# Layer trunk on one core: the dense product with V replaced by gathers of V's rows, beside gathers of U's rows

## The chip, the cores and the metric

One core of a Trainium2 chip. The metric is the device time of one execution in microseconds; the kernel before took 3484.92 us (median of 3 runs, 3472.05 to 3491.17). The engines are TensorE (PE, with its weight loads PEld), VectorE (DVE), ScalarE (ACT), GpSimd (POOL) and SyncE (SP). POOL, ACT and SP issue transfers; 16 transfer engines carry them.

## What is computed

Two layers over 512 tokens of width 1024, all in float32. Layer 0 mixes tokens by latent attention, layer 1 by chunked gated linear attention; each is followed by an expert retrieval (PEER): for each token 8 heads pick 16 of 16384 experts each, that is 128 rows of a table U and the same 128 rows of a table V.

```python
def one_block(xi):                      # 128 tokens
    q = (xi @ w_query).reshape(B, T, PEER_HEADS, 2, PEER_HALF)
    s = jnp.einsum('bthcd,cnd->bthcn', q, sub_keys)
    ...                                 # top 16 of each half, top 16 of the sums: idx, gate
    u = u_tab[idx]
    h = jax.nn.gelu(jnp.einsum('bthkd,btd->bthk', u, xi), approximate=False)
    w = (gate * h).astype(xi.dtype)
    return jnp.einsum('bthk,bthkd->btd', w, v_tab[idx])
```

Each row of U or V is 4 KB; for 128 tokens and 128 picks either table gives 64 MB of rows.

## The kernel before

Tokens lie in four tiles of 128; tiles 0 and 1 are group A, tiles 2 and 3 group B. A tile of a layer goes through mixer (`mla` or `gla`), `router` (query product, top 16, `idx` and `gate`, in four quarters of two heads), U rows (`weigh`), and V rows.

**U rows.** `weigh` (L481) takes one pick k at a time: `gather` (L473) issues one indirect transfer on POOL at L475, one row of U for each of the 128 tokens, 512 KB, into a row buffer; VectorE multiplies it with the token's normed input and sums (L487). Row buffers come from `row` (L467), round robin: 10 of a pool, and, in the sparse stretches, further ones cut out of the tile `W` (`spare`).

**V rows, two ways.** Tiles 2 and 3 of both layers: `gathered` (L517) turns picks to lie along partitions, so one indirect transfer brings the 128 rows of V of one token; `at` (L528) is the list of rows, `wd` (L535) the weights of 16 tokens spread over columns, and L543 contracts rows with weights on TensorE, 2 tokens in 8 matmuls; halves of 64 tokens are copied out (L548) and added to `h` (L549). Tiles 0 and 1 of both layers: `combine` (L593) is a dense product with the whole of V. `spread` (L556) makes a 0/1 selection on VectorE (L569, L572, L575), TensorE builds a weight matrix from it in four quarters (L581), ScalarE copies it out (L584), and SP loads all of V in 128 blocks of 512 KB (L602), each contracted with the weights of both tiles (L605); the sums are added to `h` at L617.

**What sets the order.** The program is written as generators that yield an estimate of their cost; `mix` takes the one that is furthest behind its share. A scheduler then fixes each engine's order from this, with `urgent` parts first. Each engine runs its instructions in that order; POOL's gathers wait in turn on eight counters, so that eight at most are in flight. After the attention of all tiles, `trunk` (mixers, routers, dense product) runs against `tables` (U and V rows): `tables` fetches U of (0, 2) and (0, 3), gathers V of both, then U of all four tiles of layer 1, then V of (1, 2) and (1, 3); here (l, b) is layer and tile.

## Time and profile before

| | |
|---|---|
| median of 3 runs | 3484.92 us |
| profiled execution, its own time | 3496.72 us |
| its span | 3495.0 us |
| TensorE, mean granted clock | 0.833 |
| bytes moved | 1048.11 MB, 300 GB/s over the span |

How to read it. The table of stages gives the busy time of each engine in a stretch with the number of its instructions in brackets, then the granted TensorE clock, the mean busy share of the transfer engines and what they moved. The groups of instructions give the mean of one and the idle time ahead of them with what ended it. A timeline gives each instruction's start and length, and in square brackets how long its engine had been idle and what released it. On POOL an instruction's time is the issuing of a transfer, not the transfer.

### The profile page before, as it was taken

What the parts mean: (1) busy time and instruction counts of PE and PEld (TensorE: products, weight loads), DVE (VectorE), ACT (ScalarE), POOL (GpSimd) and SP (SyncE); (2) the same over time, 40 slices, a digit from 0 to 9 for tenths busy, and PEclk for the clock granted to TensorE, in tenths of its full rate; (3) what the DMA queues carried; (4) which work ended last, traced back from release to release, by engine and by line L of the source; (5) the groups of instructions that cost most, each with busy time, mean ns of one, the idle gap of its engine ahead of it and who ended that gap; (6) DMA issues with size and microseconds to landing.
All of it is one profiled execution on the core that took longest, in us unless ns stands there. A gap on an engine that the chain in (4) does not pass through costs nothing.

```text
span 3495.0 us, 43793 instructions
## 1 busy us (share of the span) xinstructions
PE 2672.3 (76%) x15940; PEld 1642.8 (47%) x15940; DVE 2054.9 (59%) x5744; ACT 683.1 (20%) x1736; POOL 1841.9 (53%) x1540
## 2 busy tenths in 40 slices
PE   6755378858999889997895577406399997999866
PEld 4635356744555553335575455405255553533211
DVE  1588997699998850000117987899999873200000
ACT  6463377211111110003013211002111110100000
POOL 0176776155555645553404566875876464242265
PEclk8868688957999889999997687756599998899978
DMA  4599998668888989998836789997899888587698
GB/s 142 179 373 350 332 351 310 214 215 330 311 309 295 346 279 409 390 388 314 315 107 222 273 336 335 377 351 260 266 370 333 306 307 325 199 309 263 213 374 320
DMA packets 291274, 1048.11 MB, mean 300 GB/s; under 512 B 33377, under 2 KB 34913, under 8 KB 291058
## 3 DMA queue, kind: packets, MB, share of 16 engines
q0 software_dynamic: 221184, 805.40, 62.5%
q1 hardware_dynamic: 40210, 139.50, 11.0%
q10 hardware_dynamic: 29664, 100.41, 8.4%
q8 instruction: 125, 2.05, 0.2%
q14 instruction: 91, 0.75, 0.1%
HBM read 1043.09 MB, written 2.10 MB: 299 GB/s over the span
## 4 chain that ended last, share of the span: by engine, by line
PE 48%; DVE 21%; issue 12%; DMA 7%; ACT 6%; POOL 3%; another core or an unknown queue 3%; ACTq 0%; POOLq 0%; SPq 0%; DVEq 0%
PE acc L605 21%; DVE row L487 10%; PE sp L581 8%; PE mm L543 7%; PE mm L156 6%; DMA row<-in_u,idx 3%; POOL row L475 2%; DVE W L487 2%; DVE a L569 2%; DMA W<-in_v,at 1%; PE mm L396 1%; DMA row<-in_v,at 1%; DMA W<-in_u,idx 1%; POOL W L475 1%
## 5 line engine op out<-in xcount | busy, mean ns | idle before, releaser
L475 POOL DMA_INDIRECT row<-in_u,idx x927 | 1226.1, 1323 | 839.7 <-DVE idx L456 229.1
L487 DVE SCALAR_TENSOR_TENSOR row<-row,xnf 128x1024 f32<-128x1024 f32 x927 | 1111.6, 1216 | 42.5 <-DMA row<-in_u,idx 39.6
L605 PE MATMUL acc<-V,W 128*128 128x512 f32 x2048 | 1002.6, 640 | 9.8 <-DMA V<-in_v 7.6
L605 PEld LDWEIGHTS acc<-V,W 128*128 128x128 f32 x2048 | 404.4, 206 | 518.3 <-issue 503.6
L581 PE MATMUL sp<-bw,a 128*128 128x32 bf16 x6144 | 426.1, 242 | 270.7 <-DVE bw L575 109.6
L581 PEld LDWEIGHTS <-a 128*128 128x128 bf16 x6144 | 413.3, 157 | 366.8 <-issue 229.6
L475 POOL DMA_INDIRECT row<-in_v,at x373 | 360.0, 965 | 368.2 <-PE mm L543 239.9
L584 ACT ACTIVATE W<-sp 128x256 f32<-128x256 f32 x256 | 157.7, 616 | 1063.2 <-PE sp L581 855.2
L535 DVE TENSOR_TENSOR wd<-wT,same 128x512 f32<-128x512 f32 x32 | 22.0, 691 | 558.0 <-PE mm L543 362.7
L569 DVE TENSOR_TENSOR a<-rows,iotat 128x1024 bf16<-128x1024 bf16 x256 | 175.7, 687 | 238.8 <-PE sp L581 189.1
L543 PE MATMUL mm<-row,wd 128*32 128x512 f32 x1492 | 265.5, 624 | 50.7 <-DMA row<-in_v,at 35.4
L156 PE MATMUL mm<-ws,xT 128*128 128x128 f32 (+1 forms) x1920 | 253.9, 294 | 20.5 <-issue 13.2
L156 PEld LDWEIGHTS mm<-ws,xT 128*128 128x128 f32 x1920 | 244.1, 208 | 39.4 <-issue 27.8
L475 POOL DMA_INDIRECT W<-in_v,at x139 | 132.3, 952 | 231.1 <-PE acc L605 131.3
L475 POOL DMA_INDIRECT W<-in_u,idx x97 | 123.4, 1272 | 198.2 <-issue 143.6
L543 PE MATMUL mm<-W,wd 128*32 128x512 f32 x556 | 130.2, 658 | 41.0 <-issue 28.6
L543 PEld LDWEIGHTS mm<-row,wd 128*32 128x32 f32 x1492 | 49.4, 110 | 206.1 <-issue 169.7
L396 PE MATMUL mm<-xTf,ws 128*128 128x128 f32 x1024 | 139.8, 300 | 7.2 <-ACT qTf L399 5.3
L396 PEld LDWEIGHTS mm<-xTf,ws 128*128 128x128 f32 x1024 | 136.9, 216 | 10.9 <-ACT qTf L399 5.9
L575 DVE TENSOR_TENSOR bw<-e,parts 128x768 bf16<-128x768 bf16 x256 | 139.6, 550 | 0.0
L487 DVE SCALAR_TENSOR_TENSOR W<-W,xnf 128x1024 f32<-128x1024 f32 x97 | 115.8, 1215 | 3.4 <-DMA W<-in_u,idx 3.3
L402 PE MATMUL mm<-skT,qTf 128*128 128x256 f32 x128 | 40.4, 439 | 73.1 <-ACT qTf L399 58.3
(244 smaller groups left out, 2397.6 us busy)
## 6 DMA issues: line engine op xcount, KB each, us to landing
V<-in_v SPq DMA_DIRECT2D x256, 512.0 KB
ws<-in_w_query ACTq DMA_DIRECT2D x56, 512.0 KB
ws<-in_w_in ACTq DMA_DIRECT2D x48, 512.0 KB
row<-in_u,idx POOLq DMA_INDIRECT x927
ws<-in_m_w_o ACTq DMA_DIRECT2D x24, 512.0 KB
ws<-in_g_w_o ACTq DMA_DIRECT2D x16, 512.0 KB
ws<-in_w_down ACTq DMA_DIRECT2D x15, 512.0 KB
ws<-in_w_uq ACTq DMA_DIRECT2D x24, 288.0 KB
```

What stands on the lines that cost most here:

```text
L156: nc.tensor.matmul(ps, xT[:, k, :], w[:, k, :], start=(k == 0), stop=(k == kc - 1))
L396: nc.tensor.matmul(ps[:, i * P : (i + 1) * P], w[i][:, k, :], xT[b][:, k, :], start=(k == 0), stop=(k == KC - 1))
L402: nc.tensor.matmul(ps[:, i * 256 : (i + 1) * 256], qT[:, i, :], skT[l], start=True, stop=True)
L475: nc.gpsimd.indirect_dma_start(out=t, out_offset=None, in_=tab, in_offset=bass.IndirectOffsetOnAxis(ap=idx[:, k : k + 1], axis=0))
L487: nc.vector.scalar_tensor_tensor(t, t, 1.0, xn, op0=ALU.mult, op1=ALU.mult, accum_out=dots[:, k : k + 1])
L535: nc.vector.tensor_tensor(wd, w[:, s0 : s0 + TS, :].unsqueeze(3).broadcast_to([P, TS, 2, TG]), same[:, s0 : s0 + TS, :].unsqueeze(2).broad ...
L543: nc.tensor.matmul(acc[g : g + TG, :], wd[:, s, c, :], rw[c][:, n * 512 : (n + 1) * 512], start=(s0 + s == 0), stop=(s0 + s == TG - 1))
L569: nc.vector.tensor_tensor(a2, rows[:, 1, ts_].unsqueeze(1).broadcast_to([P, NK, BT]), vp_["iota"], op=ALU.is_equal)
L575: nc.vector.tensor_tensor(bw, e1.unsqueeze(1).broadcast_to([P, 3, QB, BT]), parts[:, :, ts_].unsqueeze(2).broadcast_to([P, 3, QB, BT]), op ...
L581: nc.tensor.matmul(ps[:, t * QB : (t + 1) * QB], a2[:, :, t], bw[:, j, :, t], start=(j == 0), stop=(j == 2))
L584: nc.scalar.activation(wq[:, :, o : o + BT].rearrange("p j t -> p t j"), ps.rearrange("p (t j) -> p t j", t=BT), AF.Copy)
L605: nc.tensor.matmul(acc[b, n], wq[:, c, i * P : (i + 1) * P], vt[:, n * 512 : (n + 1) * 512], start=(q + c == 0), stop=(q == NQ - 1 and c = ...
```

## The change

`combine`, `spread`, `prefill` and `in_parts` are gone, with V's dense blocks and the selection tiles. All eight (layer, tile) pairs go through `gathered`. `tables` runs three stretches: V of (0, 0), (0, 1) beside U of (0, 2), (0, 3) at shares 2 to 1; V of (0, 2), (0, 3) beside U of (1, 0), (1, 1) at 1 to 1; U of (1, 2), (1, 3) beside V of layer 1's four tiles. A generator that has nothing ready now yields `None` and is passed over in `mix`. The row pool has 16 buffers in place of 10 after the attention, and six spare ones beside the mixer's arena, 22 in all; 9 during the attention. The normed input `xnf` has three buffers.

```diff
-ROW_D, ROW_S, SPB = 1.85, 1.5, 1.65
-NROW = 10
+ROW, SPB = 1.42, 1.65
+NROW, MROW = 9, 16
...
-            xn[b] = rp.tile([P, D], F32, tag="xn", name="xnf", bufs=2)
+            xn[b] = rp.tile([P, D], F32, tag="xn", name="xnf", bufs=3)
...
-        i = turn[0] % (NROW + len(spare))
+        i = turn[0] % ((MROW if spare else NROW) + len(spare))
...
     def mix(*gens):
         live = [[g, n, 0] for g, n in gens]
         while live:
-            s_ = min(live, key=lambda z: z[2] / z[1])
-            try:
-                c = next(s_[0])
+            late = []
+            for s_ in sorted(live, key=lambda z: z[2] / z[1]):
+                try:
+                    c = next(s_[0])
+                except StopIteration:
+                    live.remove(s_)
+                    break
+                if c is None:
+                    late.append(s_)
+                    continue
                 s_[2] += c
+                for z in late:
+                    z[2] = max(z[2], s_[2] / s_[1] * z[1])
                 yield c
-            except StopIteration:
-                live.remove(s_)
+                break
+            else:
+                yield None
...
     def trunk():
-        yield from prefill(0, A)
-        yield from mix((combine(0, A), TM), (route(0, [3]), 0.6 * TM))
-        sparse_open(W_GLA)
+        spares(W_GLA)
         gla_s["gw"] = Arena()
         free[:] = [f"acc{i}" for i in range(4)]
-        yield from chain(onward(1, A), urgent(route(1, A)))
-        yield from chain(onward(1, B), urgent(route(1, [2])))
...
-        yield from prefill(1, A)
-        yield from mix((combine(1, A), TM), (urgent(route(1, [3])), 0.2 * TM))
-        sparse_open(0)
+        yield from urgent(route(0, [3]))
+        for group in (A, B):
+            yield from until(lambda: all((0, b) in summed for b in group))
+            yield from urgent(linear(group))
+            yield from urgent(route(1, group if group is A else group[:1]))
+        yield from urgent(route(1, B[1:]))
 
     def tables():
-        yield from chain(fetch(0, B), gathered(0, 2), gathered(0, 3))
-        yield from chain(fetch(1, A), fetch(1, B), gathered(1, 2), gathered(1, 3))
+        yield from mix((chain(gathered(0, 0), gathered(0, 1)), 2), (fetch(0, B), 1))
+        yield from mix((chain(gathered(0, 2), gathered(0, 3)), 1), (fetch(1, A), 1))
+        yield from mix((fetch(1, B), 1), (chain(*[gathered(1, b) for b in A + B]), 1))
```

POOL's order where the attention ends. In the names, `row` is a buffer of the row pool, `W` a spare one; `in_u` and `in_v` are the tables, `idx` and `at` the lists of rows. Before:

```order
6 L475 DMA row<-in_u,idx 128x1024 x505
7 L475 DMA W<-in_v,at 128x1024
8 L475 DMA row<-in_u,idx 128x1024 x7
9 L475 DMA row<-in_v,at 128x1024 x5
10 L475 DMA W<-in_v,at 128x1024
```

and now:

```order
6 L475 DMA row<-in_u,idx 128x1024 x256
7 L475 DMA row<-in_v,at 128x1024 x2
8 L475 DMA W<-in_v,at 128x1024 x4
9 L475 DMA row<-in_u,idx 128x1024
10 L475 DMA row<-in_v,at 128x1024 x2
11 L475 DMA row<-in_u,idx 128x1024
12 L475 DMA row<-in_v,at 128x1024
```

After 256 U rows (tiles 0 and 1) there came 256 more; now six V rows, then two V rows to one U row for 378 gathers.

POOL's order now, round the end of U of tile 3, layer 0 (the 128 U rows before), and the first U rows of layer 1:

```order
307 L475 DMA row<-in_u,idx 128x1024 x14
308 L475 DMA W<-in_v,at 128x1024 x2
309 L475 DMA row<-in_v,at 128x1024
310 L475 DMA W<-in_v,at 128x1024 x3
311 L475 DMA row<-in_v,at 128x1024 x15
312 L475 DMA W<-in_v,at 128x1024 x3
313 L475 DMA row<-in_v,at 128x1024
314 L475 DMA W<-in_v,at 128x1024 x3
315 L475 DMA row<-in_u,idx 128x1024 x2
316 L475 DMA row<-in_v,at 128x1024 x2
```

Between the last V row of tile 1 and the first U row of layer 1 (row 315) POOL has 128 U rows and 29 V rows.

POOL's order now, from the last U row of layer 1's tile 1 to the first of its tile 2:

```order
565 L475 DMA row<-in_u,idx 128x1024 x2
566 L475 DMA row<-in_v,at 128x1024 x25
567 L475 DMA W<-in_v,at 128x1024 x6
568 L475 DMA row<-in_v,at 128x1024 x16
569 L475 DMA W<-in_v,at 128x1024 x6
570 L475 DMA row<-in_v,at 128x1024 x5
571 L475 DMA W<-in_v,at 128x1024 x6
572 L475 DMA row<-in_v,at 128x1024 x26
573 L475 DMA W<-in_v,at 128x1024 x6
574 L475 DMA row<-in_v,at 128x1024 x4
575 L475 DMA W<-in_v,at 128x1024 x3
576 L475 DMA row<-in_u,idx 128x1024
```

103 V rows of tile 0, layer 1, stand between the two. The program's last 150 gathers are V rows alone.

VectorE's order now, where the last U row of tile 3, layer 0, has been weighed (L498 closes the tile):

```order
1274 L744 COPY_PREDICATED at_5303<-keep,mm 128x128
1275 L485 SCALAR_TENSOR_TENSOR row,dots<-row,xnf 128x1024 x12
1276 L498 TENSOR_TENSOR dots<-dots,gate 128x128
1277 L749 SCALAR_TENSOR_TENSOR W<-state_5311,W,mm 128x256
1278 L749 SCALAR_TENSOR_TENSOR state_5311<-W,mm 128x256
```

The mixer of layer 1 stands there between the U rows (L485 was L487); before, its first half stood beside V rows alone.

## Rows read from the trace of the kernel before

**Rows 1.** Page, costliest groups: busy us, mean ns of one, idle before.

```profile
L475 POOL DMA_INDIRECT row<-in_u,idx x927 | 1226.1, 1323 | 839.7 <-DVE idx L456 229.1
L487 DVE SCALAR_TENSOR_TENSOR row<-row,xnf 128x1024 f32<-128x1024 f32 x927 | 1111.6, 1216 | 42.5 <-DMA row<-in_u,idx 39.6
L605 PE MATMUL acc<-V,W 128*128 128x512 f32 x2048 | 1002.6, 640 | 9.8 <-DMA V<-in_v 7.6
L581 PE MATMUL sp<-bw,a 128*128 128x32 bf16 x6144 | 426.1, 242 | 270.7 <-DVE bw L575 109.6
L475 POOL DMA_INDIRECT row<-in_v,at x373 | 360.0, 965 | 368.2 <-PE mm L543 239.9
...
L569 DVE TENSOR_TENSOR a<-rows,iotat 128x1024 bf16<-128x1024 bf16 x256 | 175.7, 687 | 238.8 <-PE sp L581 189.1
```

**Rows 2.** Table of stages: stretch, engines' busy us (instructions), clock, transfer share, GB/s.

```profile
156.00:605.00 449.00, 282.20 (x1473) 213.92 (x1474) 396.47 (x1124) 246.87 (x766) 325.14 (x254) 0.76 0.93 343
...
1833.00:1876.00 43.00, 31.78 (x232) 30.64 (x233) 23.22 (x142) 19.09 (x43) 0.00 (x0) 0.88 0.31 93
...
3170.00:3291.00 121.00, 121.00 (x317) 48.19 (x310) 2.29 (x4) 0.00 (x0) 8.45 (x9) 1.00 0.53 185
3291.00:3478.00 187.00, 119.65 (x454) 24.86 (x453) 8.73 (x12) 2.37 (x4) 121.86 (x128) 0.78 0.95 360
3478.00:3495.00 17.00, 10.06 (x74) 3.51 (x73) 1.22 (x1) 1.18 (x2) 1.07 (x2) 0.98 0.39 147
```

**Rows 3.** Timelines of POOL and VectorE: start us, us, engine, line, idle before.

```profile
1645.41 0.94 POOL L475 DMA_INDIRECT W<-in_v,at  x1 [0.30 <-issue]
...
2821.85 1.22 DVE L487 SCALAR_TENSOR_TENSOR row<-row,xnf 128x1024 f32<-128x1024 f32 x1
...
2822.47 1.40 POOL L475 DMA_INDIRECT row<-in_u,idx  x1 [2.45 <-DVE e L572]
```

**Rows 4.** Transfer view, 1340 to 1440 us in 40 slices.

```profile
GB/s 410 411 408 413 408 408 401 410 410 411 411 408 410 410 408 411 410 410 411 403 410 410 410 410 408 408 387 225 288 282 318 305 383 408 419 416 403 415 408 408
```

**Rows 5.** Timeline of VectorE, 681 to 2213 us: indices, sums, decay, states.

```profile
681.56 0.18 DVE L456 SCALAR_TENSOR_TENSOR idx<-sel 128x32 int32<-128x32 bf16 x1
...
1567.84 0.69 DVE L617 TENSOR_TENSOR h<-h,acc 128x512 f32<-128x512 f32 x1 [0.17 <-PE acc L605]
...
1614.60 0.69 DVE L787 SCALAR_TENSOR_TENSOR W<-mm,W 128x512 f32<-128x512 f32 x1 [4.30 <-ACT W L785]
...
1744.96 0.48 DVE L826 SCALAR_TENSOR_TENSOR state<-W,mm 128x256 f32<-128x256 f32 x1 [2.84 <-PE mm L831]
...
1788.12 0.48 DVE L826 SCALAR_TENSOR_TENSOR state<-W,mm 128x256 f32<-128x256 f32 x1 [4.73 <-PE mm L831]
...
1798.23 0.48 DVE L826 SCALAR_TENSOR_TENSOR state<-W,mm 128x256 f32<-128x256 f32 x1
...
1832.45 0.69 DVE L174 TENSOR_TENSOR h<-h,mm 128x512 f32<-128x512 f32 x1 [3.11 <-PE mm L156]
...
1875.35 0.18 DVE L456 SCALAR_TENSOR_TENSOR idx<-sel 128x32 int32<-128x32 bf16 x1
...
1977.99 0.68 DVE L787 SCALAR_TENSOR_TENSOR W<-mm,W 128x512 f32<-128x512 f32 x1
...
2043.49 0.47 DVE L826 SCALAR_TENSOR_TENSOR state<-W,mm 128x256 f32<-128x256 f32 x1
...
2095.45 0.48 DVE L826 SCALAR_TENSOR_TENSOR state<-W,mm 128x256 f32<-128x256 f32 x1 [1.10 <-PE mm L831]
...
2212.20 0.68 DVE L174 TENSOR_TENSOR h<-h,mm 128x512 f32<-128x512 f32 x1
```

**Rows 6.** Timelines of POOL and VectorE at the program's end.

```profile
3297.92 0.94 POOL L475 DMA_INDIRECT W<-in_v,at  x1 [5.11 <-DVE at L528]
...
3478.43 0.94 POOL L475 DMA_INDIRECT W<-in_v,at  x1 [0.30 <-issue]
...
3490.12 1.22 DVE L549 TENSOR_TENSOR h<-h,W 64x1024 f32<-64x1024 f32 x1 [20.02 <-ACT W L548]
```

More of the change, by code (lines that the diff above doesn't have):

```diff
@@ L477, in gather @@
         return t
-    dense = []
     def weigh(l, b, xn, idx, gate, sel):
@@ L488, in weigh @@
                                            accum_out=dots[:, k : k + 1])
-            yield ROW_D if dense else ROW_S
+            yield ROW
         fetched.add((l, b))
@@ L544, in gathered @@
                                              start=(s0 + s == 0), stop=(s0 + s == TG - 1))
-                    yield 2 * (ROW_D if dense else ROW_S)
+                    yield 2 * (ROW)
             o = row()
@@ L552, in tile_trunk @@
     done, fetched, routed, summed = {}, set(), set(), set()
-    wqs, split, sps = {}, {}, []
-    def spread(l, group, q):
-        wq = vp_["W"][:, (q + 1) % 2]
-        wqs[l, group[0]].append(wq)
-        for b in group:
-            if q == 0:
-                while (l, b) not in fetched:
-                    yield 0.5
-                split[l, b] = in_parts(l, b)
-            rows, parts = split[l, b]
-            for t0 in range(0, P, BT):
-                ts_ = slice(t0, t0 + BT)
-                a2 = vp_["o"].tile([P, NK, BT], BF, tag="a2", name="a2", bufs=3)
-                nc.vector.tensor_tensor(a2, rows[:, 1, ts_].unsqueeze(1).broadcast_to([P, NK, BT]), vp_["iota"],
-                                        op=ALU.is_equal)
-                e1 = vp_["o"].tile([P, QB, BT], BF, tag="e1", name="e1", bufs=3)
-                nc.vector.tensor_tensor(e1, rows[:, 0, ts_].unsqueeze(1).broadcast_to([P, QB, BT]),
-                                        vp_["iota"][:, q * QB : (q + 1) * QB, :], op=ALU.is_equal)
-                bw = vp_["o"].tile([P, 3, QB, BT], BF, tag="bw", name="bw", bufs=3)
-                nc.vector.tensor_tensor(bw, e1.unsqueeze(1).broadcast_to([P, 3, QB, BT]),
-                                        parts[:, :, ts_].unsqueeze(2).broadcast_to([P, 3, QB, BT]), op=ALU.mult)
-                sps.append(sps.pop(0))
-                ps = sps[-1]
-                for t in range(BT):
-                    for j in range(3):
-                        nc.tensor.matmul(ps[:, t * QB : (t + 1) * QB], a2[:, :, t], bw[:, j, :, t],
-                                         start=(j == 0), stop=(j == 2))
-                o = (b - group[0]) * P + t0
-                nc.scalar.activation(wq[:, :, o : o + BT].rearrange("p j t -> p t j"),
-                                     ps.rearrange("p (t j) -> p t j", t=BT), AF.Copy)
-                yield SPB
@@ L588, in prefill @@
-    def prefill(l, group):
-        wqs[l, group[0]] = []
-        yield from spread(l, group, 0)
-    def combine(l, group):
-        acc = {(b, n): vp_["ps"].tile([P, 512], F32, tag=f"acc{2 * i + n}", name="acc")
-               for i, b in enumerate(group) for n in range(2)}
-        def blocks(q, wq):
-            for c in range(QB):
-                r0 = (q * QB + c) * P
-                vt = vp_["g"].tile([P, D], F32, tag="V", name="V", bufs=3)
-                nc.sync.dma_start(vt, v_tab[l][r0 : r0 + P, :])
-                for i, b in enumerate(group):
-                    for n in range(2):
-                        nc.tensor.matmul(acc[b, n], wq[:, c, i * P : (i + 1) * P],
-                                         vt[:, n * 512 : (n + 1) * 512], start=(q + c == 0),
-                                         stop=(q == NQ - 1 and c == QB - 1))
-                yield 1.72 * len(group)
-        w = wqs[l, group[0]]
-        dense.append(l)
-        ns, nb = len(group) * P // BT * SPB, QB * 1.72 * len(group)
-        for q in range(NQ):
-            yield from mix((blocks(q, w[q]), nb), *([(urgent(spread(l, group, q + 1), SOON), ns)] if q + 1 < NQ else []))
-        for b, n in acc:
-            hs = h[b][:, n * 512 : (n + 1) * 512]
-            nc.vector.tensor_tensor(hs, hs, acc[b, n], op=ALU.add)
-        summed.update((l, b) for b in group)
-        dense.clear()
@@ L621, in dense_open @@
     def dense_open():
         vp_["ps"] = ctx.enter_context(tc.tile_pool(name="ps", bufs=1, space=PSUM))
-        t = vp_["ps"].tile([P, 2, BT * QB], F32, name="sp")
-        sps.extend(t[:, i] for i in range(2))
-        vp_["g"] = ctx.enter_context(tc.tile_pool(name="gb", bufs=NROW))
+        vp_["g"] = ctx.enter_context(tc.tile_pool(name="gb", bufs=MROW))
         w = ctx.enter_context(tc.tile_pool(name="w", bufs=1))
@@ L629, in dense_open @@
         vp_["o"] = ctx.enter_context(tc.tile_pool(name="o", bufs=2))
-        t = vp_["o"].tile([P, NK, BT], BF, name="iotat", bufs=1)
-        nc.vector.tensor_copy(t, iota.unsqueeze(2).broadcast_to([P, NK, BT]))
-        vp_["iota"] = t
     def mix(*gens):
@@ L656, in fetch @@
             while (l, b) not in routed:
-                yield 0.5
+                yield None
             yield from weigh(l, b, *picks[b])
```

29 lines of the change are left out of this document (6 added, 23 removed).

## Prediction

> **What bounds the kernel now.** I read the table of stages first [rows 2], then the groups of instructions [rows 1], then the waits. Two stretches are the dense product of V (the rows of L605 and L581). The last stretch is half empty: between 3170 and 3291 us the V gathers stop, POOL is busy 8.45 of 121 us and the transfer engines stand at 0.53, because VectorE sits in order behind the end of the dense product. Everywhere else the rows of U and V come through one queue, GpSimd's (POOL), one 512 KB gather at a time, each row at L475. So three things can set the pace there: POOL's issuing, the transfer engines, and whoever frees the rows.
>
> POOL: a gather takes 0.94 us and the next one starts 0.30 us later [rows 3], 1.24 us in all. V gathers stay there in the mean (965 ns), U gathers do not (1323 ns) [rows 1]. Why is seen at 2822.47 us: the gather begins while VectorE's multiply of a U row (L487, 1216 ns) is running, and takes 1.40 us; it ends at 2823.87, 0.80 us after the multiply's end (2821.85 + 1.22 = 2823.07) [rows 3]. So a U row costs POOL 1.323 + 0.30 = 1.62 us, a V row 0.965 + 0.30 = 1.265 us. Transfer engines: where they are full they move 408 to 413 GB/s [rows 4], 524288 B in 1.28 us. That is within 2% of POOL's price of a V row and 21% below that of a U row: in a mix POOL, not the transfers, is the pacer.
>
> **What is removed.** 256 loads of V (134 MB), the 2048 matmuls of L605 (1002.6 us of TensorE), the 6144 of L581, and on VectorE L569 (175.7 us) with its two neighbours L572 and L575 [rows 1]. What replaces them is 512 more gathers, 268 MB: the total rises by 134 MB. None of the removed work is worth its busy time; it is worth the time at which the gathers run without it.
>
> **The new order, step by step.** The order of POOL's 2048 gathers is fixed in the program (the rows of order ahead show its three turns; the counts below are from it). Until the first U row of tile 2, layer 0, nothing moves: that row waits for its index at 681.56 us [rows 5], and in between only six V rows are new. I keep 682 us; one row buffer fewer there (9 for 10) I cost at nothing, since eight gathers are in flight at most by the counters they wait on.
> 1. 378 gathers, 250 of V (tiles 0, 1) and 128 of U (tile 2): 250 x 1.265 + 128 x 1.62 = 524. At the start seven quarters of routing stand on VectorE among the first 18 U rows. A quarter costs 12 us there (23.2 us for two in the stretch 1833 to 1876) [rows 2], so 84 + 18 x 1.3 = 107 us, in which POOL gets 54 rows and some 20 buffers on: a loss of 20. Where V goes to a new tile, its list of rows (`at`, one buffer) waits for the last gather of the old one; before it cost 5.11 us in POOL's row at 3297.92 [rows 6]; three U rows cover some of it: 6. End: 682 + 20 + 524 + 6 = 1232.
> 2. Layer 1's mixer of tiles 0 and 1 can start when their V rows are summed, 12 us after the last gather (3478.43 to 3490.12) [rows 6]: 1244. It runs beside 128 U rows (tile 3) and 29 V rows, 128 x 1.62 + 29 x 1.265 = 245 us of POOL. Then POOL's next instruction is a U row of layer 1, whose index needs the mixer and the router. The leg was, before: 47 us from the sum to the decay (1567.84 to 1614.60), 218 from there to the new h under V rows, 234 under U rows (1977.99 to 2212.20), and 43 from h to the first index (1832.45 to 1875.35) [rows 5]. With U rows beside it I take 47 + 234 + 43 = 324: 1568. POOL is ready at 1477 and stands 91 us.
> 3. 489 gathers, 256 U (layer 1, tiles 0 and 1) and 233 V: 256 x 1.62 + 233 x 1.265 = 710, and 10 for routing and the change of tile: 2288. V's last row of tile 3 lies 32 gathers earlier (26 of them U, 50 us), so the second mixer starts at 2288 - 50 + 12 = 2250.
> 4. Its leg, beside V rows: 47 + 218 + 43 = 308, so 2558. POOL has only 103 V rows for it, 130 us, and 182 us if the 54 MB of rows and the 21 MB of weights fill the transfer engines. It stands some 90 us again.
> 5. 509 gathers, 256 U and 253 V: 735, with 15 for routing and 8 for the lists: 3316. Then 150 V rows alone. Before, 128 of these took 187 us [rows 2], 1.461 each: 219, so 3535. From the last gather to the end 17 us [rows 2]: 3552.
> The profiled span was 3495.0, so +57 us, 1.6%. Its execution was 3496.7 and the median of three 3484.9; I put the difference on the median: **3542 us**.
>
> What the change saves is there (no dense product, no gap before 3291) but is paid for twice: 512 more gathers at 1.27 to 1.62 us, and two legs of some 300 us on the path, each with work for POOL for only 180 to 245. A 1% change of the price of a mixed row moves the result by 20 us, and break-even lies at 1.39 us for the mean of the three mixed stretches (57 us over 1376 gathers), where I have 1.43.
>
> **A rule weighed.** At 2822.47 the gather was late by what was left of one multiply [rows 3], and in the mean a U gather is late by 0.36 us of a multiply of 1.22 [rows 1]. The Trainium skill (SBUF — State Buffer, "SBUF: two separate sides") has VectorE and GpSimd take the shared port pair as an exclusive lock for a whole instruction, so that the loser fully blocks. The trace agrees on the single instruction. If every multiply shut POOL out for its whole length, a U row would cost 1.265 + 1.216 = 2.48 us; the stretch of U alone from 156 to 605 us shows 449 / 254 = 1.77 with everything in it [rows 2], so the mean goes by the row.
> The same skill (DMA: Bandwidth & Descriptors, "Where 436 GB/s comes from") says that about 358 GB/s of HBM per core binds. The trace does not agree: 410 [rows 4]. By 358 a gather could not be under 1.46 us.
>
> **Rivals.**
> - The transfers pace, not POOL. If U and V rows mixed leave the multiplies time to fall beside POOL's pauses, every stretch goes at 1.28 us: 484 for 524, 626 for 710, 652 for 735, 192 for 219, together 234 less: 3308. For it: from 156 to 605 us, with U rows alone, the transfer engines stood at 0.93 [rows 2]; against: weights went through them there too, and POOL's mean over U rows is 1.323 [rows 1]. Chance 0.11.
> - The legs shrink. In the first mixer one head followed the other by 43 us while V rows were in TensorE's queue (state at 1744.96 and 1788.12) and by 10 once they were gone (1798.23) [rows 5]. If the first leg, which has few V rows, lost most of this, and the second some, 100 us go: 3442. Against: with U rows two heads were 52 us apart (2043.49, 2095.45) [rows 5]. Chance 0.14.
> - The slow side: POOL's rows cost what the whole stretches show, waits for late multiplies and late matmuls included: 1.77 for U (156 to 605) and 1.461 for V [rows 2]. Then step 1 is 592, step 3 793, step 5 823, +239: 3781. It decides wherever a row buffer comes back late, and 22 buffers are 30 us of slack. Against: those U rows ran beside VectorE work at 88% of the time. Chance 0.07.
> - The lock in full: 0.86 us more on 640 U rows on the path, +550: 4092. Chance 0.02.
> - My sum, with the prices of a mixed row between 1.36 and 1.50 and the legs +-25 us: 3450 to 3640. Chance 0.66.
>
> **How the numbers follow.** About 0.5% (17 us) is what a measurement of this kernel can tell from no change. Faster, under 3467: 0.11 + 0.14 + 0.02 of my own case, 0.27. Within: 0.13 of my case. Slower, over 3502: 0.51 + 0.07 + 0.02, 0.60. The range leaves out the first rival (0.11) and the two on the slow side (0.09): 3400 to 3690.
>
> **What would show it.** Right: POOL's gathers at 1.36 to 1.45 us in the two-table stretches with the transfer engines under 0.95 full; POOL standing 60 to 120 us before the first U row of layer 1 and again before that of tile 2; a last stretch of V alone at about 1.4. Wrong: full transfer engines (410 GB/s) through the mixed stretches; no stand of POOL at those two places; or stands of POOL for row buffers, named after VectorE's multiply or V's matmul, spread over the mixed stretches.

## The result, and the profile after

In the batch that timed both kernels the changed one took 3620.39 us (median of 4, 3612.01 to 3630.81) and the one before 3487.19 (3472.05 to 3491.17): a ratio of 1.0391, 95% interval 1.0356 to 1.0427. The forecast had the direction right, and its range holds the time; its size was off: 57 us more were forecast, 133 measured. A later batch with the same two kernels gave 1.0093 (1.0058 to 1.0128). Both results hold, and telling why they differ is most of what follows.

The stages of the changed kernel by the table of windows (columns: stretch in us, its length, busy us and instructions of each engine, granted clock of TensorE, busy share of the transfer engines, GB/s). The first, third and fifth are the stretches of mixed rows, the second and fourth the mixers from the decay to the new h, the sixth V rows alone, the last the end:

```profile
668.00:1222.00 554.00, 329.87 (x1087) 54.73 (x1087) 231.90 (x690) 15.46 (x37) 411.33 (x379) 0.74 0.96 361
1253.00:1550.00 297.00, 197.36 (x1274) 154.13 (x1273) 160.41 (x306) 31.07 (x74) 167.35 (x138) 0.78 0.81 302
1591.00:2314.00 723.00, 355.99 (x1110) 69.10 (x1109) 394.53 (x992) 40.18 (x80) 542.16 (x488) 0.65 0.95 356
2303.00:2579.00 276.00, 239.49 (x1592) 162.37 (x1592) 40.51 (x98) 32.11 (x76) 108.61 (x110) 0.90 0.75 272
2624.00:3377.00 753.00, 388.41 (x1044) 50.80 (x1042) 386.90 (x960) 11.66 (x25) 573.42 (x508) 0.63 0.95 353
3379.00:3592.00 213.00, 141.12 (x553) 33.24 (x554) 12.26 (x18) 2.96 (x6) 142.03 (x149) 0.80 0.96 368
3592.00:3610.00 18.00, 10.99 (x56) 3.86 (x55) 1.22 (x1) 1.18 (x2) 0.94 (x1) 0.71 0.41 166
```

These answer to [rows 2]. The dense product is gone, and with it the half-empty stretch before 3291. The two legs are read on VectorE's timeline, as in [rows 5]: the last sum of V (L533), the second decay (L710), the new h (L174), the first index (L456). Here the first leg (with its last two rows from further on), then the second:

```profile
1227.31 1.22 DVE L533 TENSOR_TENSOR h<-h,row 64x1024 f32<-64x1024 f32 x1 [0.70 <-ACT row L532]
1253.42 0.69 DVE L710 SCALAR_TENSOR_TENSOR W<-mm,W 128x512 f32<-128x512 f32 x1 [2.42 <-issue]
1549.76 1.29 DVE L174 TENSOR_TENSOR h<-h,mm 128x512 f32<-128x512 f32 x2 [6.90 <-PE mm L156]
1590.28 0.18 DVE L456 SCALAR_TENSOR_TENSOR idx<-sel 128x32 int32<-128x32 bf16 x1
...
2271.89 1.22 DVE L533 TENSOR_TENSOR h<-h,row 64x1024 f32<-64x1024 f32 x1
2302.94 0.69 DVE L710 SCALAR_TENSOR_TENSOR W<-mm,W 128x512 f32<-128x512 f32 x1 [3.73 <-issue]
2579.05 0.69 DVE L174 TENSOR_TENSOR h<-h,mm 128x512 f32<-128x512 f32 x1 [3.11 <-PE mm L156]
2623.53 0.18 DVE L456 SCALAR_TENSOR_TENSOR idx<-sel 128x32 int32<-128x32 bf16 x1
```

363 us (1227.3 to 1590.3) and 352 us (2271.9 to 2623.5). POOL's timeline shows what hangs on them: its queue stands at the first U row of layer 1, and again at the first of tile 2:

```profile
1590.73 0.94 POOL L475 DMA_INDIRECT row<-in_u,idx  x1 [65.61 <-DVE bf L447]
2623.98 1.00 POOL L475 DMA_INDIRECT row<-in_u,idx  x1 [81.83 <-DVE a L444]
```

That much was foreseen. What was not is in TensorE's list of waits (line and what it waited for: us, times, longest):

```profile
PE mm L527 <- issue: 201.7, 198, 5.3
PE mm L156 <- issue: 58.7, 50, 3.2
```

"Issue" is time in which the engine waited for nothing that the profile shows: 260 us of it, before V's matmuls and the mixer's. The same list of the kernel before has far less:

```profile
PE mm L543 <- issue: 43.1, 55, 2.2
PE mm L156 <- issue: 13.2, 22, 1.1
```

On the timeline of TensorE in the first leg such a stand looks like this:

```profile
1319.16 0.27 PE L156 MATMUL mm<-ws,xT 128*128 128x128 f32 x1 [0.33 <-issue]
1320.58 0.56 PE L156 MATMUL mm<-ws,xT 128*128 128x128 f32 x1 [1.15 <-issue]
1322.67 0.37 PE L156 MATMUL mm<-ws,xT 128*128 128x128 f32 x1 [1.53 <-issue]
1324.10 0.37 PE L156 MATMUL mm<-ws,xT 128*128 128x128 f32 x1 [1.06 <-issue]
1326.89 0.37 PE L156 MATMUL mm<-ws,xT 128*128 128x128 f32 x1 [2.42 <-issue]
1329.69 0.37 PE L156 MATMUL mm<-ws,xT 128*128 128x128 f32 x1 [2.43 <-issue]
```

The matmuls start 1.42, 2.09, 1.43, 2.79 and 2.80 us apart, about 2, 3, 2, 4 and 4 times 0.70. None is missing from the record: the mixer's matmuls of this line number 1024 in each leg of both kernels. From 1315 to 1353 only 33 of them run. The granted clock there is 0.56, but a matmul still takes 0.37 us, so the clock does not make the gaps. I call this a stand of TensorE below.

TensorE is not alone in it. POOL's list of waits in the result has 85.5 us that end by "remote", that is by no instruction on record:

```profile
POOL W L475 <- remote: 48.1, 22, 5.5
POOL row L475 <- remote: 37.4, 23, 5.2
```

The kernel before has 32.2 us of them.

### The profile page after: what moved, and what is told of

It is laid out like the page before. It is cut to its first block, busy times and chain, and to the rows that moved or that the text cites. A ratio compares the mean times of both kernels' runs of the same rounds, so it can differ in the third digit from the quotient of the medians.

```text
span 3610.2 us, 31336 instructions
## 1 busy us (share of the span) xinstructions
PE 2179.7 (60%) x9796; PEld 944.7 (26%) x9796; DVE 1781.7 (49%) x4999; ACT 528.4 (15%) x1489; POOL 2300.4 (64%) x2052
## 3 DMA queue, kind: packets, MB, share of 16 engines
q8 instruction: 77, 1.26, 0.1%
## 4 chain that ended last, share of the span: by engine, by line
issue 19%; PE 12%; DMA 10%; POOL 10%; DVE 5%; another core or an unknown queue 0%; ACT 0%; POOLq 0%; ACTq 0%; DVEq 0%
POOL row L475 7%; PE mm L527 7%; DMA row<-in_v,at 5%; PE mm L156 3%; POOL W L475 3%; DMA row<-in_u,idx 2%; DMA W<-in_v,at 2%; DMA W<-in_u,idx 1%; DVE row L485 1%; PE mm L396 1%; DVE W L485 0%; DVE tiu L370 0%; DVE s L368 0%; DVE tiu L367 0%
## 5 line engine op out<-in xcount | busy, mean ns | idle before, releaser
L527 PE MATMUL mm<-row,wd 128*32 128x512 f32 x2972 | 1007.2, 850 | 780.5 <-DMA row<-in_v,at 606.5
L475 POOL DMA_INDIRECT row<-in_u,idx x816 | 972.6, 1192 | 617.6 <-issue 201.8
L485 DVE SCALAR_TENSOR_TENSOR row<-row,xnf 128x1024 f32<-128x1024 f32 x816 | 982.8, 1221 | 569.6 <-DMA row<-in_u,idx 422.8
L475 POOL DMA_INDIRECT row<-in_v,at x743 | 797.4, 1073 | 362.7 <-issue 191.5
L527 PEld LDWEIGHTS mm<-row,wd 128*32 128x32 f32 x2972 | 144.2, 127 | 1560.9 <-DMA row<-in_v,at 1025.4
L527 PE MATMUL mm<-W,wd 128*32 128x512 f32 x1124 | 387.5, 823 | 209.5 <-DMA W<-in_v,at 147.5
L475 POOL DMA_INDIRECT W<-in_v,at x281 | 301.4, 1073 | 211.0 <-PE mm L527 94.5
L485 DVE SCALAR_TENSOR_TENSOR W<-W,xnf 128x1024 f32<-128x1024 f32 x208 | 252.0, 1224 | 140.6 <-DMA W<-in_u,idx 120.4
L156 PE MATMUL mm<-ws,xT 128*128 128x128 f32 (+1 forms) x1920 | 263.6, 297 | 58.7 <-issue 58.2
L475 POOL DMA_INDIRECT W<-in_u,idx x208 | 228.8, 1100 | 101.3 <-issue 50.6
L156 PEld LDWEIGHTS mm<-ws,xT 128*128 128x128 f32 x1920 | 251.9, 212 | 81.0 <-issue 77.0
L527 PEld LDWEIGHTS mm<-W,wd 128*32 128x32 f32 x1124 | 57.8, 128 | 461.0 <-DMA W<-in_v,at 270.0
L485 DVE DVE_READ_ACCUMULATOR row<-row,xnf 128x1 f32 x816 | 66.4, 81 | 0.2 <-issue 0.2
L156 PE MATMUL mm<-ws,oT 128*128 128x128 f32 x512 | 61.5, 279 | 6.1 <-DMA ws<-in_m_w_o 4.0
L156 PEld LDWEIGHTS mm<-ws,oT 128*128 128x128 f32 x512 | 59.3, 194 | 8.3 <-DMA ws<-in_m_w_o 4.7
```

The costliest lines, as they stand in the source:

```text
L156: nc.tensor.matmul(ps, xT[:, k, :], w[:, k, :], start=(k == 0), stop=(k == kc - 1))
L475: nc.gpsimd.indirect_dma_start(out=t, out_offset=None, in_=tab, in_offset=bass.IndirectOffsetOnAxis(ap=idx[:, k : k + 1], axis=0))
L485: nc.vector.scalar_tensor_tensor(t, t, 1.0, xn, op0=ALU.mult, op1=ALU.mult, accum_out=dots[:, k : k + 1])
L527: nc.tensor.matmul(acc[g : g + TG, :], wd[:, s, c, :], rw[c][:, n * 512 : (n + 1) * 512], start=(s0 + s == 0), stop=(s0 + s == TG - 1))
```

## Two conditions: the same kernels, with and without TensorE's stands

Kernels of one batch ran on one chip, and the kernel before was timed in each. It tells two sorts of batch apart: it takes 3479 to 3487 us, the result among them, or 3369. I name them by what their profiles show, **with stands** and **without**.

The first repetition of both kernels (no edit):

> The changed kernel as it is, once more. In its first profile TensorE stood 202 us in front of the matmuls of V rows and 59 us in front of the mixer's, waiting for nothing that the profile shows; in the kernel before these were 43 and 13 us, and in the four experiments so far none. Theory A (the stands belong to that run, not to the kernel's order): here they are under 20 us, the mixed stretches take some 1.38 us a row, the legs some 315 and 300 us, and the kernel is 0.5 to 2% slower than the one before, about 1.6% as forecast. Theory B (they belong to the kernel): 150 us or more of such stands, legs of 350 us or more, and 3 to 4.5% slower.

> The kernel before as it is, for its profile beside the others of this call. Theory A: no stands of TensorE without a cause, its V rows alone at the end at 1.27 to 1.30 us each, where its first profile had 1.46 in the whole stretch. Theory B: some 40 to 70 us of such stands as in the first profile, V rows alone at 1.4 or more.

This batch fell without stands. Changed kernel 3395.23 us, before 3368.69, ratio 1.0093 (1.0058 to 1.0128). TensorE's issue waits in the changed kernel are down to one, and the kernel before has no row of them:

```profile
PE mm L527 <- issue: 0.5, 1, 0.5
```

The same stages of the changed kernel in this batch (mixed, mixer, mixed, mixer, mixed, V alone):

```profile
667.00:1183.00 516.00, 304.12 (x1087) 48.46 (x1081) 230.47 (x688) 15.42 (x37) 396.72 (x379) 0.82 1.00 387
1214.00:1466.00 252.00, 184.94 (x1273) 147.15 (x1273) 161.61 (x306) 30.97 (x74) 163.63 (x135) 0.85 0.92 356
1505.00:2193.00 688.00, 361.06 (x1153) 70.61 (x1153) 395.10 (x996) 43.01 (x86) 538.59 (x489) 0.66 0.98 374
2180.00:2413.00 233.00, 221.04 (x1591) 147.38 (x1591) 40.56 (x98) 32.15 (x77) 109.07 (x111) 0.99 0.86 323
2458.00:3173.00 715.00, 378.43 (x1043) 48.87 (x1041) 391.43 (x962) 11.90 (x25) 555.77 (x510) 0.63 0.98 373
3173.00:3370.00 197.00, 145.61 (x577) 23.21 (x577) 12.47 (x20) 2.95 (x6) 140.29 (x149) 0.91 1.00 396
```

Every stage is shorter: the mixed ones by 38, 35 and 38 us, the mixers by 45 and 43, the end of V alone by 16. The program and POOL's order are the same. POOL has no wait for "remote" any more, in either kernel. Theory A is borne out, with the loss near the low end of its 0.5 to 2%. In its single run before_again took 3367.59 us (span 3365.8, against 3495.0) with 1.31 us a row for its last 128 V rows, where it had 1.46, so the kernel before gains 129 us of span and the changed one 224.

The unedited kernel again, in later batches:

> The changed kernel as it is, a third time, as the one to compare with in this call. If TensorE's stands without a recorded cause come and go with the run, this shows either none and a span near 3386, or more than 150 us of them and one near 3610.

> The changed kernel as it is, to see what holds in this call. Theory: the two outcomes go with the chip, which the kernel before tells too: near 3370 us it has none of TensorE's stands and the changed kernel is near 3390; near 3485 us it has some 60 us of them and the changed kernel 200 or more, near 3620. Rival (they go with the single run): a mixture, the one without the other.

3640.12 us where the kernel before took 3485.41 (median), and 3605.64 where it took 3478.82; L527 stood 165.0 and 164.5 us on issue, L156 35.9 and 37.1, and POOL's waits for "remote" were 81.6 and 85.9 us. So the stands come in every batch in which the kernel before is the slower one, and in no other: they go with the batch, and as a batch is one chip, probably with the chip (13, in two batches, and 14 with stands, 4 and 7 without; the result's is not on record). They are no chance of a single run.

What the stands need, in a batch that has them:

```diff
# e9_half: half of each row gathered, used twice
+        n //= 2
         t = row()[:, :n]
# e10_split: each matmul of a V row in two of 256 columns
-  matmul(acc[g:g+TG, :], wd[:, s, c, :], rw[c][:, n*512:(n+1)*512], ...)
+  for q in range(2):
+    matmul(acc[g:g+TG, q*256:(q+1)*256], wd[:, s, c, :], rw[c][:, n*512+q*256 : n*512+(q+1)*256], ...)
```

> The changed kernel with gathers of half a row (2 KB of 4 KB of each row), the first half multiplied or contracted twice; it leaves the other half of U and V out. As many gathers and TensorE instructions, half the bytes. Theory (TensorE's stands need full transfers): where the changed kernel shows them, they are under 30 us here. Rival (they go with the number of its instructions): they stay over 150 us. In any case the mixed stretches show POOL's own price with a half multiply: 1.25 to 1.30 us a row if POOL paces at 0.94 + 0.30.

> The changed kernel with each matmul of a V row cut in two of 256 columns, twice as many TensorE instructions for the same rows. Theory (the stands are a shortage of instructions at TensorE): where the changed kernel shows 200 us of them, 350 or more here, and the kernel is 100 us longer; where it shows none, none here and within 40 us of it. Rival (they go with the bytes or the time): as many as in the changed kernel, and within 40 us of it.

TensorE's issue waits before V's matmuls in its list of waits, all of one batch. The unedited kernel, after_fourth:

```profile
PE mm L527 <- issue: 164.5, 204, 5.7
```

With half rows, e9_half (V's matmuls stand one line lower there):

```profile
PE mm L528 <- issue: 239.9, 260, 3.2
```

With the matmuls split, e10_split:

```profile
PE mm L528 <- issue: 387.0, 426, 3.8
```

Half the bytes (183 to 187 GB/s in the mixed stretches, transfer engines at 0.63 to 0.64; the kernel took 3575.60 us) take nothing away: full transfers are not the cause. The price that I had named for that run, 1.25 to 1.30 us a row, did not come either: its second and third mixed stretch cost 1.43 and 1.44. Twice the matmuls of V rows bring 2.4 times the stands there (387.0 to 164.5), so in this order they grow with the number of TensorE's instructions; the kernel took 3673.28 us, 68 more than its neighbour, where I had expected 100. The number alone does not set them, though: e8_sixteen below has the same instructions and fewer row buffers, and 91.3 us for 165.0. A shortage of instructions is thus not shown, and what makes TensorE and POOL stand in some batches stays open. The page's row of instruction transfers reads `q8 instruction: 77, 1.26` (packets, MB) for the changed kernel in both conditions, at 0.1 and 0.2% of the transfer engines' time, so more of them is not what differs.

## The legs: what lengthens them

```diff
# e2_quiet: the rows that ran beside a leg are gathered after it (tables(), same rows in all)
+  mix(((V00, V01), 2), (fetch(0, [2]), 1));  fetch(1, [0])
+  mix(((V02, V03), 2), (fetch(0, [3]) then fetch(1, [1]), 2));  fetch(1, [2])
+  mix((fetch(1, [3]), 1), (all V of layer 1, 3))
# e3_nomul03: multiply of U rows of tile 3, layer 0, over 8 columns
+  n = 8 if (l, b) == (0, 3) else D
```

(V02 stands for gathered(0, 2), and so on.) Both without stands.

> The changed kernel with the gathers that stand beside the two legs moved behind them: the next gather of POOL is in both cases a row that needs the leg's result, so a leg runs with nothing beside it. Theory (what runs beside a leg makes it long: VectorE's multiplies in front of its steps, V rows in TensorE's queue, and a TensorE clock that falls while it waits): from the last sum of V (L533) to the first index 220 us or less, against 363 and 352 in the changed kernel, TensorE's clock 0.9 or more in the leg; POOL stands all of it, so the whole is longer, some 3780. Rival (the leg's own chain of steps is that long): 330 us or more in the quiet too, and some 4000 for the whole.

> The changed kernel in which the multiply of U rows of tile 3, layer 0, which run beside the first leg, takes 8 of 1024 columns; the gathers stay. It leaves out most of these 128 dot products. Theory A (VectorE's queue holds the first leg up: the multiplies stand in front of its steps, TensorE waits and loses its clock): the first leg falls from 363 us to 310 or less. Theory B (full transfers or TensorE's own queue hold it up): it stays at 345 or more. The second leg stays at 352 by both.

**e2_quiet**: 3652.93 us (3780 expected, by prices with stands). From sum to index 217 us (1198.95 to 1416.43) and 224 us, for 220 or less. The two mixers, decay to h, with nothing beside them:

```profile
1222.00:1377.00 155.00, 150.53 (x1164) 133.18 (x1164) 24.31 (x72) 28.45 (x70) 0.00 (x0) 0.99 0.34 103
2362.00:2518.00 156.00, 151.99 (x1163) 134.47 (x1164) 24.33 (x72) 28.00 (x69) 0.00 (x0) 0.98 0.33 102
```

TensorE is busy 97% at a granted clock of 0.99 and 0.98, and the two are alike. In the changed kernel without stands they take 252 and 233, the first at a granted clock of 0.85: what runs beside a mixer costs it 77 to 97 us. That something beside a leg makes it long holds; which of the theory's three causes it is, this run can't tell.

**e3_nomul03**: the first leg took 317 us, between the two bounds (310 or less, 345 or more), which I had set from the result's 363. The second leg, which the edit doesn't touch and which should have stayed at 352, fell to 300 as well: this batch was without stands, where the unedited kernel's legs are 317 and 307 us. So 128 multiplies less on VectorE moved the first leg by nothing that shows, and theory A falls. Only the untouched leg told this; the edited place alone, 363 to 317, would have seemed to speak for theory A.

Depth of the pool, one part of the change undone, then more:

```diff
-NROW, MROW = 9, 16
+NROW, MROW = 9, 10     # e8_sixteen: 16 buffers in all; e6_few has 6: 12 in all
```

> The changed kernel with 6 instead of 16 buffers beside the 6 spare ones, 12 for the 22. Theory (eight gathers are in flight at most and a row is free some 2 us after it landed, so 12 are enough but for blocks behind the routing and the mixer's steps): up to 60 us longer, all of it in the legs and in the first rows after them. Rival (the 22 carry the mixed stretches): 1.55 us a row or more in the mixed stretches, 150 us longer.

> The changed kernel with 10 instead of 16 buffers beside the 6 spare ones, 16 for the 22: the part of the change that adds buffers is undone. Theory (a deeper pool lets more landed rows queue in front of the mixer's steps on VectorE and TensorE): the legs lie between those with 22 (317 and 307 us) and with 12 (284 and 272), the span between 3386 and 3336, about 3365. Rival (with 12 the order of the program merely fell better): no shortening, 3386 or more.

**e6_few** (without stands): 3337.82 us, 57 *less* than the changed kernel, where I had expected up to 60 more. Legs of 284 and 272 us for 317 and 307; the mixed stretches 1.39 to 1.41 us a row for 1.37 to 1.41. TensorE's waits in the first mixer, first those of after_again:

```profile
PE mm L527 <- DMA W<-in_v,at: 23.6, 2, 13.7
PE mm L138 <- DVE at L744: 16.9, 2, 11.1
PE mm L742 <- DVE W L749: 13.8, 3, 12.6
PE mm L138 <- DVE W L732: 9.1, 1, 9.1
```

Then those of e6_few:

```profile
PE mm L138 <- DVE at L744: 7.1, 2, 4.8
PE mm L742 <- DVE W L749: 5.7, 3, 4.4
PE mm L138 <- DVE W L732: 4.3, 2, 3.7
```

The waits for VectorE fall from 40 to 17 us and the wait for a V row goes. The order of the two engines shows why. With 22 buffers 104 of V's matmuls stand among the first mixer's on TensorE, with 12 none (424 and 322 in the second mixer). On VectorE 116 U rows stand between the first mixer's second decay and its last state, with 12 buffers 91. What a mixer's step waits for there is not the multiplies, as e3_nomul03 shows: it has the order of the changed kernel without these multiplies, and TensorE's three waits for VectorE are 40 us all the same (17.0, 14.4 and 8.4). VectorE waits for the rows to land instead, from sum to new h in e3_nomul03 and in after_again:

```profile
DVE row L486 <- DMA row<-in_u,idx: 100.7, 70, 2.6
...
DVE row L485 <- DMA row<-in_u,idx: 19.5, 26, 1.5
```

So a step stands in VectorE's fixed order behind rows that come one by one. In e3_nomul03 they landed 1.28 us apart where the transfers were full (409 GB/s from 1254 to 1270 us); 25 rows fewer would be 32 us, by estimate, and the first leg is 33 shorter.

**e8_sixteen** (with stands): 3545.01 us against 3640.12, legs of 309 and 319 for 363 each, TensorE's issue waits before V rows 91.3 us for 165.0. The legs are shorter, as the theory has it, but its cause isn't shown here: the order is nearly that of 22 buffers (104 and 432 of V's matmuls in the mixers, 108 U rows), and the stands are fewer. Both depths are single runs. The 22 buffers thus cost 57 us against 12 without stands, and 61 to 95 against 16 with them (3605.64 and 3640.12 are the two single runs of the changed kernel); I had counted them only as slack.

## The legs filled

```diff
# e1_fill
+  mix(((V00, V01), 1), (fetch(0, B), 1));  V02, V03, fetch(1, A)
+  mix(((V10, V11), 1), (fetch(1, B), 1));  V12, V13
# e5_nomix: one table at a time, the rows beside both legs are U
+  V00, V01, fetch(0, B);  V02, V03, fetch(1, A)
+  V10, V11, fetch(1, B);  V12, V13
# e7_both: e1_fill, 12 buffers.   nomix_few: e5_nomix, 14 buffers
```

> The changed kernel with another order of the gathers: V rows of tiles 0 and 1 of layer 0 beside U rows of tiles 2 and 3, then V rows of tiles 2 and 3 alone, then U rows of layer 1 for tiles 0 and 1 alone, then V rows of tiles 0 and 1 beside U rows of tiles 2 and 3, then V rows of tiles 2 and 3. Both mixer legs now have 256 gathers beside them, where the changed kernel has some 157 and 103. Theory (the price of a row is what I forecast, and the loss is two legs of some 355 us of which POOL can fill only a part): first U row of tile 2 at 668, 512 mixed rows at 1.45 = 742, sum 12, first leg beside 256 V rows at 1.405 = 360, second leg beside 256 U rows at 1.77 = 453, 512 mixed rows at 1.48 = 758, 256 V rows at 1.405 = 360, end 18: a span of about 3370, with no stand of POOL over 30 us in front of the first U row of layer 1 or of tile 2. Rival 1 (a leg grows with the rows beside it): the legs take 450 each, POOL stands again some 90 us twice, about 3550. Rival 2 (the price of the mixed rows is the whole loss, the legs cost nothing): within 30 us of the changed kernel's 3610.

> The filled legs once more, beside the changed kernel on the same chip. If the loss is POOL standing in front of the two legs (66 and 82 us) and U alone in part of them, it is 110 to 190 us under the changed kernel in the same call; if a leg grows as much as it is filled, less than 60.

> The filled legs a third time, in case the call falls where TensorE's stands without a recorded cause come (the kernel before near 3485 us). Theory (POOL standing in front of the legs is the one part of the loss, the stands the other): there it is 110 to 190 us under the changed kernel's 3610 to 3640, so about 3470, level with the kernel before. Rival (filling the legs takes the stands away too, since TensorE has slack again): 3350 or less. Where the stands do not come it repeats 3256 against 3369.

**Without stands** e1_fill took 3258.19 us, ratio to the kernel before 0.9663 (0.9637 to 0.9689), e1_again 3256.18, 0.9676 (0.9642 to 0.9709), 139 us under the changed kernel of the same batch, where 110 to 190 was expected. (The 3370 expected of e1_fill came from prices with stands, and can't be held against these.) Legs of 327 and 371 us, but POOL doesn't stand: the first U row of layer 1 and that of tile 2, in e1_again:

```profile
1720.25 0.94 POOL L475 DMA_INDIRECT row<-in_v,at  x1 [0.30 <-DMA row<-in_v,at]
...
2179.25 0.94 POOL L475 DMA_INDIRECT row<-in_u,idx  x1 [0.30 <-DVE tv L366]
```

(The first is the V row that is being fetched when the index comes.) The two stands of POOL, 65 and 82 us in after_again, go: 139 us are gained against their 147. **With stands** e1_third took 3510.99 us, 1.0083 (1.0056 to 1.0111), 95 under its neighbour after_fourth, short of the 110 to 190, and its span of 3511.7 is 142 over the 3370 that I had worked out with such prices. It lies above the kernel before, since V rows beside a mixer then wait for TensorE (legs of 418 and 399 us; POOL waits 104.4 us for L527 in the first, 23.9 in e1_again). TensorE's issue waits before L527 stay at 153.8 us; filling doesn't cure the stands.

> The changed kernel with each table's rows alone, no stretch of V beside U: V of tiles 0 and 1, U of 2 and 3, V of 2 and 3, U of layer 1 for 0 and 1, V of 0 and 1, U of 2 and 3, V of 2 and 3. Each leg has 256 U rows beside it, and POOL does not stand. By rows of the second profile (V alone 1.27 to 1.30 a row, U alone 1.60): 658 + 4 x 256 x 1.29 + 3 x 256 x 1.60 + 18 = 3226, with some 40 for the steps at both ends of a leg 3270, that is 115 under the changed kernel. Rival 1 (U and V beside each other are what makes rows cheap): alone they are dearer than in the ends of the stretches, 3330 or more. Rival 2 (the two legs beside U grow to 400 and POOL stands again): 3330 or more too, but with stands over 30 us in front of the first row of layer 1.

> The order without mixing once more, timed. Where TensorE's stands come it took 3421 us, some 60 under the kernel before. Theory (its gain is that POOL never stands in front of a leg and that V rows stay out of the legs, on any chip): 0.96 to 0.985 of the kernel before, near 3420 against 3480 or 3270 against 3370. Rival (it gains only where TensorE's stands make mixed rows dear): level with the kernel before where these stands are missing.

> The order without mixing with 14 in place of 22 buffers. Theory (fewer landed rows queue in front of the mixer's steps, but POOL has rows beside the legs anyway): within 15 us of the 22. Rival (a shorter leg lets the next stretch start with the index ready, as in the mixed order with 12): 30 us or more less.

> Filled legs with 12 buffers in place of 22. Theory (in the filled order POOL no longer stands in front of a leg's result, so a shorter leg brings nothing): within 20 us of the filled legs' 3248 to 3264. Rival (fewer buffers help by themselves, in the mixed stretches too): 40 us or more less, about 3210.

All with stands. e5_nomix 3420.89 us, 219 less than the changed kernel beside it; timed again 3407.06, 0.9807 (0.9755 to 0.9860). The 3270 expected were worked out without stands and stay untested. It beats both kernels where e1 does not, although TensorE stands 249.2 and 260.4 us on issue before its V rows. In blocks of 64 rows V alone costs 1.38 to 1.56 us (1.73 in one block behind an index), U alone beside no leg 1.37 to 1.64, so a mixed row, 1.47 to 1.50 in after_third, is no cheaper than the two apart; what is gained is the order, without a stand of POOL and without V rows in the mixers. So nothing here speaks for my rival 1. nomix_few: 3418.08, 0.9812 (0.9757 to 0.9867); its legs are 347 and 331 us for 413 and 408, and it brings nothing, since POOL has rows anyway. e7_both: 3502.51, 1.0035 (1.0013 to 1.0058), level with e1_third at legs of 326 and 322 us for 418 and 399. In these two orders a shorter leg does not pay, as POOL does not stand behind it. How e5_nomix does without stands was not run.

## The price of a row

```diff
# e4_nomul: the multiply of every U row over 8 of 1024 columns
-  scalar_tensor_tensor(t, t, 1.0, xn, ...)
+  scalar_tensor_tensor(t[:, :8], t[:, :8], 1.0, xn[:, :8], ...)
```

> The changed kernel in which the multiply of every U row takes 8 of 1024 columns; all gathers stay. It leaves out most of the dot products of U. Theory A (POOL's issuing paces the mixed stretches, and a U row costs more only since VectorE's multiply delays the gather): the mixed stretches go from 1.43 to 1.57 us a row to 1.30, so 1375 rows save about 230 us, the legs some 50, the span is 3330 or less. Theory B (the transfers, 0.95 busy in the mixed stretches, are the pace at 355 GB/s whatever VectorE does): 1.45 or more a row stays, and the span is 3520 or more.

3252.87 us, without stands, 142 under the changed kernel in that condition; 34 of it come ahead of the first U row of tile 2 (632 us for 667), from the multiplies beside the attention. Its POOL rows of U and V among the groups of instructions (line, engine, operation, count, busy us, mean ns):

```profile
L475 POOL DMA_INDIRECT row<-in_u,idx x816 | 777.6, 953 | 736.9 <-issue 159.6
L475 POOL DMA_INDIRECT row<-in_v,at x743 | 703.9, 947 | 289.6 <-issue 166.6
```

The same rows of after_again:

```profile
L475 POOL DMA_INDIRECT row<-in_u,idx x816 | 941.8, 1154 | 600.1 <-issue 188.8
L475 POOL DMA_INDIRECT row<-in_v,at x743 | 782.2, 1053 | 316.2 <-issue 179.0
```

So multiplies cost a U gather 0.20 us and a V gather beside them 0.11; together close to the 0.36 that I had put on U alone. The second and third mixed stretch fall from 1.41 and 1.40 us a row to 1.30 and 1.31. The first, with two V rows to one U row, does not (1.37 to 1.36): without stands its transfer engines stood at 1.00 already. Nor do the legs (317 and 299 us), where I had expected some 50 less. In the second and third stretch the transfers now pace, by the table of windows:

```profile
1468.00:2104.00 636.00, 338.14 (x1090) 64.34 (x1089) 129.42 (x993) 40.19 (x80) 465.56 (x490) 0.70 1.02 404
2368.00:3035.00 667.00, 362.02 (x1037) 48.52 (x1035) 124.67 (x961) 11.88 (x25) 484.51 (x509) 0.66 1.01 398
```

Theory A holds for these two stretches: the 0.98 at 373 and 374 GB/s of the unedited kernel in this condition (0.95 at 353 and 356 in the result) was not the transfers' limit; they went on to 398 and 404. The Trainium skill (SBUF — State Buffer, "SBUF: two separate sides") has the shared port as an exclusive lock, between a VectorE instruction with two inputs in SBUF and one of GpSimd that reads SBUF: the loser is fully blocked for the other's whole instruction. The trace agrees, gather by gather. In after_again:

```profile
1217.33 1.21 DVE L485 SCALAR_TENSOR_TENSOR row<-row,xnf 128x1024 f32<-128x1024 f32 x1
...
1217.38 1.97 POOL L475 DMA_INDIRECT row<-in_u,idx  x1 [0.30 <-issue]
```

The gather ends 0.81 us after the multiply, as the one of [rows 3] did (0.80). On the timelines of that whole run a gather that begins with 0.4 to 0.6 us of a multiply left takes 1.32 us in the mean, with 0.8 to 1.0 left 1.71, with no multiply beside it 0.95. The mean cost is only 0.20 since 586 of the 2048 gathers begin with more than 0.2 us of a multiply left.

## Why the prediction was wrong in size

Its terms against the profile of the result and the one without stands, in us:

| term | forecast | result | without stands |
|---|---|---|---|
| first U row of tile 2 | 682 | 668 | 667 |
| step 1, 378 gathers | 550 | 554 | 516 |
| step 2, first leg | 324 | **363** | 317 |
| step 3, 489 gathers | 720 | 725 | 688 |
| step 4, second leg | 308 | **352** | 307 |
| step 5, 509 gathers | 758 | 755 | 715 |
| 150 V rows alone | 219 | 214 | 197 |
| end | 17 | 18 | 16 |

- **Steps 2 and 4 failed.** In the result the legs are 39 and 44 us longer than my terms, 83 in all; the earlier start (14) and smaller differences take back 25 of it, and 58 is what the span is over my 3552. The part that failed is the mixer from the decay to the new h: 297 and 276 us for 234 and 218. TensorE's issue waits before L156 in the two mixers are 32.9 us (1253 to 1550) and some 25 (2303 to 2579); the rest I can't assign. I had priced the legs from [rows 5], where the kernel before had 13 us of such waits in all of L156. A leg taken over from another order carries over the waits of that order.
- **Without stands both legs are within 7 us of the forecast, by luck.** The mixers are still 18 and 15 us over my terms there (252 and 233); what makes up for it is the way from the sum to the decay, for which I had taken 47 us and which took 26 and 30.
- **Steps 1, 3 and 5 and the end held within 5 us each**, in the result, and that too is partly luck. In these stretches a U gather took 1.06 to 1.13 us where I had 1.323, and a V gather 1.10 to 1.13 where I had 0.965: of the kernel before's U gathers 50% began with over 0.2 us of a multiply left, here it is 22 to 30% of U and V alike. Beyond the 0.30 between two gathers POOL waited 29, 34 and 27 us, 49 of it for "remote". Without stands the same stretches are 34, 32 and 43 us under the forecast.
- **POOL's two stands** came where I put them, 66 and 82 us for 91 and 90: smaller, though the legs are longer, since the rows beside the first leg took 302 us (1222 to 1524) and not 245, and POOL waited for V's matmul (L527) to free a buffer in both legs, 40 and 98 us. Filling the stands is worth 95 to 139 us: more than the order loses without stands, but not all that it loses with them.
- **Row buffers.** I named stands of POOL for V's matmul spread over the mixed stretches as a sign against me. POOL waits 191 us for L527 in the result and 103 without stands, but 138 of the 191 lie in the two legs and 35 in the three mixed stretches. The sign did not come: in the legs POOL stands for the index in any case. Of the signs for me, mixed rows at 1.47 to 1.48 us with the transfers at 0.95 to 0.96 lie just outside the 1.36 to 1.45 and the "under 0.95" that I had named.
- **Rivals.** The transfers don't pace steps 3 and 5 (e4_nomul is faster there by VectorE's work alone), but without stands they do pace step 1. The legs don't shrink. The prices of whole stretches would have been far too slow. So would the full lock as I priced it, a whole multiply on every U row; but the mean, by which I set the rule aside, does not contradict the lock, which each gather shows.
- **What decides the size** is outside the sum: with stands the order loses 3.6 to 4.4%, without 0.9%. Of the 224 us between the two profiles of the changed kernel 90 lie in steps 2 and 4, 114 in the mixed stretches of steps 1, 3 and 5 and 16 in the V rows alone. I had thought that the gathered rows wait for TensorE's matmuls. In the mixed stretches that is 10 us (35 for 25); POOL's waits for "remote" are 57 there and its gathers 38 longer. That the kernel before gains less (129) since it has fewer gathers is argued, not shown.

## What to carry to other kernels

Where one queue paces a kernel, look for the places where its next instruction needs a result of a long chain, and put work that needs nothing of the chain in front of it, of the kind that doesn't share the chain's engine. More buffers are not free: they can put more rows in front of the chain's steps in an engine's fixed order. And give an experiment a control, a part that the edit can't move, and time the unedited kernel beside it.

## What the runs showed of the hardware that was not expected

- In some batches TensorE starts its matmuls only every 0.70 us or a multiple for tens of us, waiting for nothing that is recorded; in others never. POOL then waits 82 to 86 us in the changed kernel for something that is not on record, and otherwise not at all. TensorE's waits before V rows grew from 164.5 to 387.0 us for twice as many matmuls, did not fall with half the bytes (239.9), and were 91.3 for 165.0 with 16 buffers for 22.
- Transfer engines that show 0.98 busy moved 373 and 374 GB/s and did not pace; with VectorE's multiplies gone they moved 398 and 404 at 1.01 and 1.02. The busy share alone did not tell who paced.
- A gather on POOL that begins while a VectorE multiply runs ends some 0.8 us after it; where few gathers do, the mean cost is small (0.20 us of a 1.22 us multiply).
- A mixer alone ran TensorE at a granted clock of 0.98 to 0.99; with rows beside it the first one had 0.85 and the second 0.99, with stands 0.78 and 0.90.
